# Masked running sum taken at one row per batch, then a matrix product: lengths read into registers, and the sum moved to fp32 matmuls in four column groups

## The chip, the cores and the metric

One core of a Trainium2 chip runs the kernel. The metric is device time in microseconds (us) for one execution. Three runs of the kernel before gave 200.6, 201.1 and 201.49 us; the median is 201.1 us.

## What is computed

```python
B, S, D = 8, 8192, 512                     # x [B,S,D] fp32, lengths [B] int64, w [D,D] fp32
mask = (pos < lengths[:, None, None])
cs = np.cumsum(x * mask, axis=1)
mid_features = cs[np.arange(B), lengths // 2, :]
return np.matmul(mid_features[:, None, :], w).squeeze(1)
```

Only one row of each running sum is used, the one at `lengths // 2`. So for each batch the answer is the sum of the first n rows of x, n = min(lengths // 2 + 1, lengths), multiplied by w. The inputs are drawn once with a fixed seed. The lengths are 1138, 5379, 511, 4113, 1809, 7542, 7716 and 1140, so n is 570, 2690, 256, 2057, 905, 3772, 3859 and 571 for batches 0 to 7: 14,680 rows of 2 KB in all. Since lengths are below 8192, n is never above 4096 = S/2.

## The kernel before, in words

The kernel doesn't know the lengths when it is built, so it loads the first 4096 rows of every batch: 8 x 4096 rows of 2 KB, 67.1 MB. For each batch there are 8 groups, each of 4 x 128 rows. A group is one DMA of 1 MB issued by SP into `xt` (L65), in which every partition receives four separate rows of 2 KB, 128 rows apart. VectorE casts the group to bf16 in `xb` (L67), and TensorE adds it with four matmuls (L70), whose stationary operand is one column of `mask_t`: 1 for rows at or before the middle, 0 for the others. All 32 x 8 = 256 matmuls add into one row of PSUM per batch, which VectorE copies to `mf_sb` (L72). The pool `sb` has 12 buffers for each of the two tiles.

The masks are made at the start: SP loads the lengths (L41), VectorE halves them (L43, L46), GpSimd broadcasts them over the partitions (L48) and writes row numbers (L51), and VectorE compares (L55).

Behind the last batch stands a chain: the eight sums lie in one partition, so they are written to DRAM (L75) and read back transposed with eight DMAs of 4-byte elements (L78); four fp32 matmuls multiply them by w (L85), VectorE copies the result (L88) and SP writes it (L89). The order on each engine is the order of the program, and the Tile framework sets the semaphores. SP's queue holds all of the transfers in this order: lengths, the 64 groups of x, the round trip, with the four loads of w among them, and the output.

Of the kernel before, what the change touches and what calls it, by code (L numbers as in the profile page):

```python
# [1 line left out]

# [4 lines left out]


@with_exitstack
def kernel(  # L10
    ctx: ExitStack,
    tc: tile.TileContext,
    x: bass.AP,
    lengths: bass.AP,
    w: bass.AP,
    out: bass.AP,
):
    nc = tc.nc
    import concourse.bass as _b
    _b.log.warn_once_per_call_stack = lambda *a, **k: None  # L20
    ctx.enter_context(nc.allow_non_contiguous_dma(reason="meta"))
    B, S, D = x.shape
    assert D == 512 and B == 8
    SM = S // 2
    NCH = SM // 128
    G = 4
    NGRP = NCH // G

    f32 = mybir.dt.float32
    bf16 = mybir.dt.bfloat16  # L30
    f32r = mybir.dt.float32r
    i32 = mybir.dt.int32

    sb = ctx.enter_context(tc.tile_pool(name="sb", bufs=12))
    sc = ctx.enter_context(tc.tile_pool(name="sc", bufs=1))
    pp = ctx.enter_context(tc.tile_pool(name="pp", bufs=4, space=bass.MemoryType.PSUM))
    dp = ctx.enter_context(tc.tile_pool(name="dp", bufs=1, space=bass.MemoryType.DRAM))

    lens_i = sc.tile([1, 2 * B], i32)
    lsrc = lengths.tensor.reshape([B]).bitcast(i32).ap().rearrange("(o t) -> o t", o=1)  # L40
    nc.sync.dma_start(out=lens_i[:, :], in_=lsrc)  # L41
    mid_i = sc.tile([1, B], i32)
    nc.vector.tensor_scalar(out=mid_i[:], in0=lens_i[:, ::2], scalar1=1, scalar2=None,  # L43
                            op0=mybir.AluOpType.logical_shift_right)
    mid_f = sc.tile([1, B], f32)
    nc.vector.tensor_copy(out=mid_f[:], in_=mid_i[:])  # L46
    mid_bc = sc.tile([128, B], f32)
    nc.gpsimd.partition_broadcast(mid_bc[:], mid_f[:])  # L48

    iota_t = sc.tile([128, NCH], f32)  # L50
    nc.gpsimd.iota(iota_t[:], pattern=[[128, NCH]], base=0, channel_multiplier=1,  # L51
                   allow_small_or_imprecise_dtypes=True)
    mask_t = sc.tile([128, B, NCH], bf16)
    for b in range(B):
        nc.vector.tensor_scalar(out=mask_t[:, b, :], in0=iota_t[:],  # L55
                                scalar1=mid_bc[:, b:b + 1], scalar2=None,
                                op0=mybir.AluOpType.is_le)

    mf_sb = sc.tile([1, B, D], f32)
    xr = x.rearrange("b (ng g p) d -> b ng p g d", p=128, g=G)  # L60
    for b in range(B):
        ps = pp.tile([1, D], f32, tag="ps")
        for ng in range(NGRP):
            xt = sb.tile([128, G, D], f32, tag="xt")
            nc.sync.dma_start(out=xt[:], in_=xr[b, ng])  # L65
            xb = sb.tile([128, G, D], bf16, tag="xb")
            nc.vector.tensor_copy(out=xb[:], in_=xt[:])  # L67
            for g in range(G):
                c = ng * G + g
                nc.tensor.matmul(out=ps[:], lhsT=mask_t[:, b, c:c + 1], rhs=xb[:, g, :],  # L70
                                 start=(c == 0), stop=(c == NCH - 1))
        nc.vector.tensor_copy(out=mf_sb[:, b, :], in_=ps[:])  # L72

    mf_dram = dp.tile([1, B, D], f32)
    nc.sync.dma_start(out=mf_dram[:], in_=mf_sb[:])  # L75
    mf_t = sc.tile([128, 4, B], f32)
    for b in range(B):
        nc.sync.dma_start(out=mf_t[:, :, b],  # L78
                          in_=mf_dram[:, b, :].rearrange("o (kc p) -> (o p) kc", p=128))

    ps_out = pp.tile([B, D], f32)
    for kc in range(4):
        wt = sb.tile([128, D], f32)
        nc.sync.dma_start(out=wt[:], in_=w[kc * 128:(kc + 1) * 128, :])
        nc.tensor.matmul(out=ps_out[:], lhsT=mf_t[:, kc, :], rhs=wt[:],  # L85
                         start=(kc == 0), stop=(kc == 3))
    out_sb = sc.tile([B, D], f32)
    nc.vector.tensor_copy(out=out_sb[:], in_=ps_out[:])  # L88
    nc.sync.dma_start(out=out[:], in_=out_sb[:])  # L89


# [1 line left out]
_INS = ['x', 'lengths', 'w']  # L93
_OUTS = [((8, 512), 'float32')]


# [23 lines left out]
```

## Time and profile before

| | |
|---|---|
| Median of three runs | 201.1 us (200.6 to 201.49) |
| Span of the profiled execution, first to last instruction | 200.5 us; no other time of that execution is recorded |
| TensorE matmul, weight load | 113.9 us (57%), 29.1 us (14%) busy |
| VectorE | 85.4 us busy (43%) |
| Bytes moved by DMA | 68.26 MB, mean 340 GB/s |
| Mean granted TensorE clock | 0.625 of full speed |

The profile's page lists the span in 40 slices of about 5 us; a digit is the busy share of a slice in tenths. In the rows below, PE is TensorE's matmul and PEld its weight load, DVE is VectorE, POOL is GpSimd, SPq is SyncE's queue of DMA issues. The chain that ended last is followed back from the last instruction to whatever released each step.

### The profile page before, as it was taken

The numbers are of one execution on the slowest core, as the hardware profiler recorded it, in microseconds if no ns is written. First come the engines' busy times: TensorE is split into PE (matmuls) and PEld (weight loads), VectorE is DVE, ScalarE is ACT, GpSimd is POOL, SyncE is SP. The second block draws the span as 40 slices with busy tenths as digits, with TensorE's granted clock in tenths as the row PEclk, the third lists the DMA queues.
The fourth block names the chain that finished last, engine by engine and source line by source line (L and its number), as shares of the span: only waits on it lengthen the run. The fifth ranks groups of instructions, "written<-read, shape, count | busy, mean of one in ns | idle before, by whom it ended". The sixth has DMA issues, their size and how long they took to land.

```text
span 200.5 us, 853 instructions
## 1 busy us (share of the span) xinstructions
PE 113.9 (57%) x264; PEld 29.1 (14%) x264; DVE 85.4 (43%) x83; POOL 0.6 (0%) x6
## 2 busy tenths in 40 slices
PE   0004947766653756677655665764867765663093
PEld 0001311111110111111111111111211111110010
DVE  0334664344644444443644454445544364441001
POOL 0000000000000000000000000000000000000000
PEclk9999995555588555555585558555555558555558
DMA  4999999999999999999999999999999999980400
GB/s 148 367 398 386 387 387 388 387 386 386 386 389 388 385 388 386 386 386 386 386 387 386 387 387 387 386 387 388 386 386 387 384 387 386 388 312 9 3 0 3
DMA packets 38616, 68.26 MB, mean 340 GB/s; under 512 B 5323, under 2 KB 5323, under 8 KB 38611
## 3 DMA queue, kind: packets, MB, share of 16 engines
q1 hardware_dynamic: 38612, 68.21, 93.5%
q8 instruction: 2, 0.03, 0.1%
q14 instruction: 2, 0.02, 0.0%
HBM read 68.17 MB, written 0.03 MB: 340 GB/s over the span
## 4 chain that ended last, share of the span: by engine, by line
DMA 78%; SPq 11%; PE 5%; DVE 3%; issue 1%; DVEq 0%
DMA xt<-in_x_dram 76%; SPq L65 9%; PE ps_out L85 3%; DVE xb L67 2%; PE ps L70 2%; SPq L78 2%; DMA mf_t<-mf_dram 1%; DMA mf_dram<-mf_sb 1%; DVE mf_sb L72 0%; DVE out_sb L88 0%; SPq L41 0%; DVEq L67 0%
## 5 line engine op out<-in xcount | busy, mean ns | idle before, releaser
L70 PE MATMUL ps<-xb,mask_t 128*1 128x512 bf16 x256 | 107.4, 575 | 74.7 <-DVE xb L67 56.8
L67 DVE CAST xb<-xt 128x2048 bf16<-128x2048 f32 x64 | 78.2, 1224 | 77.2 <-DMA xt<-in_x_dram 77.2
L70 PEld LDWEIGHTS <-mask_t 128*1 128x1 bf16 x256 | 28.1, 110 | 153.0 <-issue 130.1
L72 DVE COPY mf_sb<-ps 1x512 f32<-1x512 f32 x8 | 5.4, 679 | 14.8 <-PE ps L70 14.8
L85 PE MATMUL ps_out<-wt,mf_t 128*8 128x512 f32 x8 | 6.6, 1000 | 8.8 <-DMA mf_t<-mf_dram 8.8
L88 DVE COPY out_sb<-ps_out 8x512 f32<-8x512 f32 x1 | 0.7, 679 | 14.7 <-PE ps_out L85 14.7
L55 DVE TENSOR_SCALAR mask_t<-iota_t,mid_bc 128x32 bf16<-128x32 f32 x8 | 1.3, 236 | 4.0 <-POOL mid_bc L48 4.0
L85 PEld LDWEIGHTS ps_out<-wt,mf_t 128*8 128x8 f32 x8 | 0.9, 126 | 14.0 <-issue 14.0
L43 DVE TENSOR_SCALAR mid_i<-lens_i 1x8 int32<-1x8 int32 x1 | 0.2, 159 | 1.9 <-DMA lens_i<-in_lengths_dram 1.9
L48 POOL PARTITION_BROADCAST mid_bc<-mid_f x1 | 0.3, 280 | 8.2 <-issue 8.2
L51 POOL IOTA iota_t<- 128x32 f32 x1 | 0.2, 157 | 8.5 <-issue 8.5
L46 DVE CAST mid_f<-mid_i 1x8 f32<-1x8 int32 x1 | 0.2, 159 | 0.0
L104 POOL MEMSET const-uint8-127<- 128x1 uint8 x1 | 0.1, 102 | 0.0
L104 POOL MEMSET const-bfloat16-1.0<- 128x1 bf16 x1 | 0.1, 101 | 0.0
L104 POOL MEMSET const-float32-0.0<- 128x1 f32 x1 | 0.1, 98 | 0.2 <-issue 0.2
L104 POOL MEMSET const-float32-1.0<- 128x1 f32 x1 | 0.1, 98 | 0.0
## 6 DMA issues: line engine op xcount, KB each, us to landing
xt<-in_x_dram SPq DMA_DIRECT2D x64, 1024.0 KB, 14.4
wt<-in_w_dram SPq DMA_DIRECT2D x4, 256.0 KB, 10.8
mf_t<-mf_dram SPq DMA_DIRECT2D x8, 2.0 KB, 2.3
lens_i<-in_lengths_dram SPq DMA_DIRECT2D x1, 0.1 KB
mf_dram<-mf_sb SPq DMA_DIRECT2D x1, 16.0 KB
out_dram<-out_sb SPq DMA_DIRECT2D x1, 16.0 KB
```

What stands on the lines that cost most here:

```text
L43: nc.vector.tensor_scalar(out=mid_i[:], in0=lens_i[:, ::2], scalar1=1, scalar2=None, op0=mybir.AluOpType.logical_shift_right)
L46: nc.vector.tensor_copy(out=mid_f[:], in_=mid_i[:])
L48: nc.gpsimd.partition_broadcast(mid_bc[:], mid_f[:])
L55: nc.vector.tensor_scalar(out=mask_t[:, b, :], in0=iota_t[:], scalar1=mid_bc[:, b:b + 1], scalar2=None, op0=mybir.AluOpType.is_le)
L65: nc.sync.dma_start(out=xt[:], in_=xr[b, ng])
L67: nc.vector.tensor_copy(out=xb[:], in_=xt[:])
L70: nc.tensor.matmul(out=ps[:], lhsT=mask_t[:, b, c:c + 1], rhs=xb[:, g, :], start=(c == 0), stop=(c == NCH - 1))
L72: nc.vector.tensor_copy(out=mf_sb[:, b, :], in_=ps[:])
L78: nc.sync.dma_start(out=mf_t[:, :, b], in_=mf_dram[:, b, :].rearrange("o (kc p) -> (o p) kc", p=128))
L85: nc.tensor.matmul(out=ps_out[:], lhsT=mf_t[:, kc, :], rhs=wt[:], start=(kc == 0), stop=(kc == 3))
L88: nc.vector.tensor_copy(out=out_sb[:], in_=ps_out[:])
L104: nc = _bacc.Bacc("TRN2", target_bir_lowering=False, num_devices=1)
```

## The change

The kernel is written anew, without the Tile framework's semaphores, between one set of hand-placed waits. SP and TensorE each load the lengths into 16 registers and work out n for every batch (`counts`). Both then walk the same code: for every batch up to eight whole blocks of 512 rows, each behind a comparison of n with a constant (`whole_blocks`), so that a block beyond n is neither loaded nor added. The rows left over, fewer than 512, are split by the binary digits of n: 256 rows, 128 rows, and the last up to 127 rows, for which 32, 64, 96 or 128 rows are loaded and those beyond n masked. With the lengths drawn there are 26 whole blocks; three loads of 256 rows (batches 2, 4, 6), three of 128 (1, 4, 5), and seven last ones (32 rows for batches 1, 3, 4 and 6, 64 for 0, 5 and 7): 39 loads of 14,784 rows, 30.28 MB. The first 26 carry 27.26 MB, the 13 others 3.01 MB.

In a block each partition now takes four neighbouring rows, one run of 8 KB. There is no cast: TensorE multiplies fp32 directly, and of the four row sets of a block each goes to its own 32-column group of the array, `tile_position=(0, 32*j)`, with eight stationary columns of which one is 1, so that batch b's sum is added to row b of the group. Afterwards the four groups are added (`fold`) by four matmuls which also transpose the sums, in place of the round trip through DRAM, and the product with w is split over the four column groups by output columns. The lengths for the masks and all of w are loaded by ACT's queue at the start. `xt` holds two batches (b % 2) of eight blocks; before SP loads over a block it waits for TensorE to have read it (`wait_free`).

```diff
+    xt = sb("xt", [P, 2, NB, G, D])
+    rem = sb("rem", [P, B, G, D])
...
+    def counts(eng):
+        regs = [eng.alloc_register(f"n_{eng.engine.name}_{i}") for i in range(2 * B)]
+        eng.load(regs, lens_words)
+        for b in range(B):
+            length, n = regs[2 * b], regs[2 * b + 1]
+            eng.reg_alu(n, length, 1, ALU.logical_shift_right)
+            eng.reg_alu(n, n, 1, ALU.add)
+            eng.reg_alu(n, n, length, ALU.min)
+        return regs[1::2], regs[0]
+
+    def whole_blocks(eng, n, body, k=0):
+        if k < NB:
+            with eng.If_cmp(n, BLK * (k + 1), "IS_GE"):
+                body(k)
+                whole_blocks(eng, n, body, k + 1)
...
+    @block.sync
+    def _(sp):
+        ns, t = counts(sp)
+        def wait_free(b, k):
+            if b >= 0:
+                with sp.If_cmp(ns[b], BLK * (k + 1), "IS_GE"):
+                    sp.wait_ge(s_free[b], k + 1)
+                with sp.Else():
+                    wait_free(b - 2, k)
+        for b in range(B):
+            def load_block(k):
+                wait_free(b - 2, k)
+                sp.dma_start(
+                    out=xt[:, b % 2, k],
+                    in_=x[b, k * BLK:(k + 1) * BLK].rearrange("(p g) d -> p g d", g=G),
+                ).then_inc(s_full[b][k], 16)
+            whole_blocks(sp, ns[b], load_block)
...
+        sp.wait_ge(s_pool, 1)
+        for b in range(B):
+            sp.reg_alu(t, ns[b], 256, ALU.bitwise_and)
+            with sp.If_cmp(t, 1, "IS_GE"):
+                sp.reg_alu(base, ns[b], ~(2 * 256 - 1), ALU.bitwise_and)
+                sp.dma_start(
+                    out=rem[:, b, 0:2],
+                    in_=rows(b, base, 256).rearrange("(p g) d -> p g d", g=2),
+                ).then_inc(s_rem[b][0], 16)
...
+        sp.wait_ge(s_dve, DVE_MASK + 3)
+        for j in range(0, 4, 2):
+            sp.dma_start(out=out[:, j * P:(j + 1) * P], in_=o_sb[32 * j:32 * j + B]).then_inc(s_out, 16)
+        sp.wait_ge(s_out, 64)
+    @block.scalar
+    def _(act):
+        act.dma_start(out=lens[:], in_=lens_words.to_broadcast((P, 2 * B))).then_inc(s_len, 16)
+        act.dma_start(out=wt[:], in_=w.rearrange("(kc p) d -> p kc d", p=P)).then_inc(s_w, 16)
...
+    @block.tensor
+    def _(pe):
+        ns, t = counts(pe)
+        def add(j, weights, rows):
+            return pe.matmul(s_ps[32 * j:32 * j + weights.shape[-1]], lhsT=weights, rhs=rows,
+                             start=False, stop=False, skip_group_check=True,
+                             tile_position=(0, 32 * j))
+        for j in range(4):
+            pe.matmul(s_ps[32 * j:32 * j + 32], lhsT=zero[:, :32], rhs=zero[:],
+                      start=True, stop=False, skip_group_check=True, tile_position=(0, 32 * j))
+        for b in range(B):
+            one = sel[:, B - 1 - b:2 * B - 1 - b]
+            def add_block(k):
+                pe.wait_ge(s_full[b][k], 16)
+                for j in range(G):
+                    mm = add(j, one, xt[:, b % 2, k, j])
+                mm.then_inc(s_free[b], 1)
+            whole_blocks(pe, ns[b], add_block)
...
+            with pe.If_cmp(t, 1, "IS_GE"):
+                pe.wait_ge(s_rem[b][2], 16)
+                add(3, mask[:, b], rem[:, b, 3])
+        for j in range(4):
+            mm = pe.matmul(s_ps[32 * j:32 * j + 32], lhsT=zero[:, :32], rhs=zero[:],
+                           start=False, stop=True, skip_group_check=True,
+                           tile_position=(0, 32 * j))
+        mm.then_inc(s_pe, 1)
+        pe.wait_ge(s_dve, DVE_MASK + 1)
+        for kc in range(KC):
+            mm = pe.matmul(mf_ps[:, kc * B:(kc + 1) * B], lhsT=s_sb[:, kc * P:(kc + 1) * P],
+                           rhs=fold[:], start=True, stop=True)
...
+        for kc in range(KC):
+            for j in range(4):
+                mm = pe.matmul(o_ps[32 * j:32 * j + B, :P], lhsT=mf_sb[:, kc],
+                               rhs=wt[:, kc, j * P:(j + 1) * P],
+                               start=(kc == 0), stop=(kc == KC - 1), tile_position=(0, 32 * j))
```

## Rows read from the trace of the kernel before

**Rows 1.** The page's 40 slices: clock, DMA share, rate.
```profile
PEclk9999995555588555555585558555555558555558
DMA  4999999999999999999999999999999999980400
GB/s 148 367 398 386 387 387 388 387 386 386 386 389 388 385 388 386 386 386 386 386 387 386 387 387 387 386 387 388 386 386 387 384 387 386 388 312 9 3 0 3
```

**Rows 2.** The page: the chain that ended last, by line.
```profile
DMA xt<-in_x_dram 76%; SPq L65 9%; PE ps_out L85 3%; DVE xb L67 2%; PE ps L70 2%; SPq L78 2%; DMA mf_t<-mf_dram 1%; DMA mf_dram<-mf_sb 1%; DVE mf_sb L72 0%; DVE out_sb L88 0%; SPq L41 0%; DVEq L67 0%
```

**Rows 3.** The page: groups (count, busy us, mean ns, idle before).
```profile
L70 PE MATMUL ps<-xb,mask_t 128*1 128x512 bf16 x256 | 107.4, 575 | 74.7 <-DVE xb L67 56.8
L67 DVE CAST xb<-xt 128x2048 bf16<-128x2048 f32 x64 | 78.2, 1224 | 77.2 <-DMA xt<-in_x_dram 77.2
```

**Rows 4.** The chain in order of time, from the last group on (start, us).
```profile
178.86 0.04 issue
178.90 1.24 DVE xb L67
180.14 0.04 issue
180.18 1.88 PE ps L70 x4
...
182.79 1.67 DMA mf_dram<-mf_sb
...
184.47 0.39 SPq L78
...
188.21 2.29 DMA mf_t<-mf_dram
190.50 0.38 issue
190.88 6.57 PE ps_out L85 x8
197.44 0.02 issue
197.47 0.68 DVE out_sb L88
```

**Rows 5.** Stretches: length, PE, PEld, DVE, POOL busy, clock, DMA share, GB/s.
```profile
2.00:3.00 1.00, 0.00 (x0) 0.00 (x0) 0.26 (x2) 0.00 (x0) 1.00 0.26 80
40.00:160.00 120.00, 76.18 (x176) 19.68 (x176) 56.51 (x49) 0.00 (x0) 0.56 1.05 387
184.50:190.50 6.00, 0.00 (x0) 0.00 (x0) 0.00 (x0) 0.00 (x0) 0.50 0.37 3
```

**Rows 6.** The tile xt: SP's issues and time to landing.
```profile
L65 SPq DMA_DIRECT2D xt<-in_x_dram x64: 407/2535/4254, 1.1 to 164.4; - x64
DMA to landing us min/median/max: 5.4/14.4/15.8
```

**Rows 7.** Timeline of the start and of the output (start, us).
```profile
0.73 0.34 SPq L41 DMA_DIRECT2D lens_i<-in_lengths_dram  x1
1.13 1.50 SPq L65 DMA_DIRECT2D xt<-in_x_dram  x3
1.95 0.16 DVE L43 TENSOR_SCALAR mid_i<-lens_i 1x8 int32<-1x8 int32 x1 [1.95 <-DMA lens_i<-in_lengths_dram]
...
198.18 0.30 SPq L89 DMA_DIRECT2D out_dram<-out_sb  x1
```

**Rows 8.** Line L85, fp32 on TensorE (ns min/median/max, first and last start).
```profile
L85 PEld LDWEIGHTS ps_out<-wt,mf_t x8: 88/138/138, 190.8 to 195.9; 128*8 128x8 f32 x8
L85 PE MATMUL ps_out<-wt,mf_t x8: 630/1061/1061, 190.9 to 196.8; 128*8 128x512 f32 x8
L85 PEldq EVENT_SEMAPHORE  x4: 51/51/51, 190.1 to 190.8; - x4
```

**Rows 9.** More stretches, columns as in rows 5, for TensorE's clock.
```profile
17.90:22.50 4.60, 4.60 (x11) 1.33 (x12) 4.35 (x10) 0.00 (x0) 1.00 1.05 386
22.90:25.90 3.00, 3.00 (x16) 1.16 (x14) 1.26 (x2) 0.00 (x0) 1.00 1.05 386
31.00:44.00 13.00, 8.93 (x21) 2.19 (x20) 6.13 (x5) 0.00 (x0) 0.50 1.05 387
190.90:197.40 6.50, 6.50 (x8) 0.90 (x8) 0.00 (x0) 0.00 (x0) 0.54 0.00 0
```

**Rows 10.** Timeline: two weight loads of the fp32 product.
```profile
191.68 0.14 PEld L85 LDWEIGHTS ps_out<-wt,mf_t 128*8 128x8 f32 x1 [0.71 <-issue]
192.54 0.14 PEld L85 LDWEIGHTS ps_out<-wt,mf_t 128*8 128x8 f32 x1 [0.72 <-issue]
```

**Rows 11.** The page: DMA queues that fetch instructions.
```profile
q8 instruction: 2, 0.03, 0.1%
q14 instruction: 2, 0.02, 0.0%
```

More of the change, by code (lines that the diff above doesn't have):

```diff
@@ L4 @@
 import concourse.tile as tile
-from concourse import bass_utils, mybir
+from concourse import mybir
 from concourse._compat import with_exitstack
+F32 = mybir.dt.float32
+I32 = mybir.dt.int32
+ALU = mybir.AluOpType
+ds = bass.ds
+P = 128
 @with_exitstack
@@ L18 @@
     nc = tc.nc
-    import concourse.bass as _b
-    _b.log.warn_once_per_call_stack = lambda *a, **k: None
-    ctx.enter_context(nc.allow_non_contiguous_dma(reason="meta"))
+    ctx.enter_context(nc.allow_non_contiguous_dma(reason="lengths"))
     B, S, D = x.shape
-    assert D == 512 and B == 8
-    SM = S // 2
-    NCH = SM // 128
     G = 4
[L27 to L86, printed above, removed]
@@ L87, with sb @@
-    out_sb = sc.tile([B, D], f32)
-    nc.vector.tensor_copy(out=out_sb[:], in_=ps_out[:])
-    nc.sync.dma_start(out=out[:], in_=out_sb[:])
+    BLK = P * G
+    NB = S // 2 // BLK
+    KC = D // P
+    STEP = 32
+    xf = x.rearrange("b s d -> (b s) d")
+    lens_words = lengths.tensor.reshape([B]).bitcast(I32).ap().rearrange("(o t) -> o t", o=1)
+    ctx.enter_context(tc.tile_critical(no_gpsimd_drain=True))
+    def sb(name, shape, dt=F32):
+        return ctx.enter_context(nc.sbuf_tensor(name, shape, dt))
@@ new lines, in ps, with sem @@
+    def ps(name, shape):
+        return ctx.enter_context(nc.psum_tensor(name, shape, F32))
+    def sem(name):
+        return tc.alloc_semaphore(name)
+    xt = sb("xt", [P, 2, NB, G, D])
+    rem = sb("rem", [P, B, G, D])
+    wt = sb("wt", [P, KC, D])
+    lens = sb("lens", [P, 2 * B], I32)
+    cnt = sb("cnt", [P, B], I32)
+    cap = sb("cap", [P, B], I32)
+    row = sb("row", [P, 1], I32)
+    mask = sb("mask", [P, B, B])
+    sel = sb("sel", [P, 2 * B - 1])
+    zero = sb("zero", [1, D])
@@ new lines @@
+    fold_i = sb("fold_i", [P, B], I32)
+    fold = sb("fold", [P, B])
+    s_sb = sb("s_sb", [P, D])
+    mf_sb = sb("mf_sb", [P, KC, B])
+    o_sb = sb("o_sb", [P, P])
+    s_ps = ps("s_ps", [P, D])
+    mf_ps = ps("mf_ps", [P, D])
+    o_ps = ps("o_ps", [P, D])
+    s_full = [[sem(f"full{b}_{k}") for k in range(NB)] for b in range(B)]
+    s_rem = [[sem(f"rem{b}_{k}") for k in range(3)] for b in range(B)]
+    s_free = [sem(f"free{b}") for b in range(B)]
+    s_w, s_len, s_out = sem("w"), sem("len"), sem("out")
@@ new lines @@
+    s_pool, s_dve, s_pe = sem("pool"), sem("dve"), sem("pe")
+    def counts(eng):
[12 more added lines that the diff above has]
+                whole_blocks(eng, n, body, k + 1)
@@ new lines, in _ @@
+    @block.scalar
+    def _(act):
+        act.dma_start(out=lens[:], in_=lens_words.to_broadcast((P, 2 * B))).then_inc(s_len, 16)
+        act.dma_start(out=wt[:], in_=w.rearrange("(kc p) d -> p kc d", p=P)).then_inc(s_w, 16)
+        act.wait_ge(s_dve, DVE_MASK + 3)
+        for j in range(1, 4, 2):
+            act.dma_start(out=out[:, j * P:(j + 1) * P], in_=o_sb[32 * j:32 * j + B]).then_inc(s_out, 16)
+    @block.gpsimd
+    def _(pool):
+        pool.memset(rem[:, :, 3], 0.0).then_inc(s_pool, 1)
+        pool.iota(row[:], pattern=[[0, 1]], base=0, channel_multiplier=1)
+        pool.iota(fold_i[:], pattern=[[-1, B]], base=128, channel_multiplier=1).then_inc(s_pool, 1)
@@ new lines, in _, with step @@
+    @block.vector
+    def _(dve):
+        done = 0
+        def step(do, *args, **kw):
+            nonlocal done
+            if done:
+                dve.wait_ge(s_dve, done)
+            do(*args, **kw).then_inc(s_dve, 1)
+            done += 1
+        step(dve.memset, zero[:], 0.0)
+        step(dve.memset, sel[:], 0.0)
+        step(dve.memset, sel[:, B - 1:B], 1.0)
+        assert done == DVE_SEL
+        step(dve.memset, mask[:], 0.0)
+        step(dve.memset, o_ps[:, :P], 0.0)
+        dve.wait_ge(s_len, 16)
+        step(dve.tensor_scalar, out=cnt[:], in0=lens[:, ::2], scalar1=1, scalar2=None,
+             op0=ALU.logical_shift_right)
+        step(dve.tensor_scalar, out=cap[:], in0=cnt[:], scalar1=1, scalar2=None, op0=ALU.add)
+        step(dve.tensor_tensor, out=cnt[:], in0=cap[:], in1=lens[:, ::2], op=ALU.min)
+        step(dve.tensor_scalar, out=cap[:], in0=cnt[:], scalar1=127, scalar2=None,
+             op0=ALU.bitwise_and)
+        dve.wait_ge(s_pool, 2)
+        step(dve.tensor_tensor, out=mask[:].rearrange("p a b -> p (a b)")[:, ::B + 1], in0=cap[:],
+             in1=row[:].to_broadcast((P, B)), op=ALU.is_gt)
+        step(dve.tensor_scalar, out=cnt[:], in0=fold_i[:], scalar1=31, scalar2=None,
+             op0=ALU.bitwise_and)
+        step(dve.tensor_scalar, out=fold[:], in0=cnt[:], scalar1=0, scalar2=None, op0=ALU.is_equal)
+        assert done == DVE_MASK
+        dve.wait_ge(s_pe, 1)
+        step(dve.tensor_copy, out=s_sb[:], in_=s_ps[:])
+        dve.wait_ge(s_pe, 2)
+        step(dve.tensor_copy, out=mf_sb[:].rearrange("p a b -> p (a b)"), in_=mf_ps[:, :KC * B])
+        dve.wait_ge(s_pe, 3)
+        step(dve.tensor_copy, out=o_sb[:], in_=o_ps[:, :P])
```

40 lines of the change are left out of this document (added).

## The prediction

> **What bounds the kernel now.** I read the page's slices first. From the second 5 us to the 35th slice the DMA engines are busy throughout at 384 to 398 GB/s [rows 1]; 120 us from the middle read 387 GB/s, while TensorE and VectorE have idle time in the same stretch [rows 5]. The chain agrees: 76% of the span is the load of x and 9% SP's queue at the same loads [rows 2], and both engines behind it wait: the casts for DMA, the matmuls for the casts [rows 3]. So the time is bytes over rate: 67.1 MB at 387 GB/s are 173.4 us. Data first flows at about 2.74 us (the share of 0.26 in the third microsecond, [rows 5]), 1.6 us after the first issue [rows 7], and the last group has landed at 178.86 us [rows 4]: 2.7 us more than rate alone gives, for the ramps. Behind it stand 21.6 us of tail to the end of the span at 200.5 us: cast, matmuls, round trip through DRAM, product, output [rows 4].
>
> All sums are made against that span; the median of the runs is 0.6 us above it, and I add that at the end.
>
> **The stream of x.** It falls from 67.1 to 30.28 MB. At the old rate this takes 78.2 us. The packets change too: a partition's share of a block is one run of 8 KB instead of four of 2 KB, which the trace doesn't show. At 387 GB/s over 16 engines a packet of 2 KB takes 84.7 ns. The round trip moves 8 x 512 elements of 4 bytes in 6 us at a DMA share of 0.37 [rows 5]: 0.37 x 16 x 6 us / 4096 = 8.7 ns each, nearly all of it cost per packet, so an upper bound of that cost. Three such costs saved make 8 KB in 4 x 84.7 - 3 x 8.7 = 313 ns, or 419 GB/s. The ends are 387 and 419; I take 410 for the 27.26 MB of whole blocks, nearer the top because the small packet is a direct row for the overhead, and 387 for the 3.01 MB of shorter rows: 66.5 + 7.8 = 74.3 us (73 to 78).
>
> Here a rule speaks against any such rate. The Trainium skill, "DMA: Bandwidth & Descriptors", section "Where 436 GB/s comes from", says that for transfers between HBM and SBUF a limit of about 358 GB/s per core binds; by it the stream would take 84.6 us and the sum would be 10 us higher. The trace contradicts it, with 387 GB/s held for 120 us.
>
> **The start.** Before the first load of x, SP now reads 16 registers from DRAM, works out eight n with 24 register operations, and compares once. No row shows a register load. The lower end is one small transfer, from the issue of the lengths at 0.73 us to VectorE's use at 1.95 us: 1.2 us [rows 7]; the upper end is one such trip for each of 16 words, 19 us. It is one instruction over 64 contiguous bytes, so nearest the single trip: 1.2 us and 16 writes of 0.05 us (a semaphore instruction took 51 ns, [rows 8]) make 2.0. The operations at 0.05 us make 1.2, the comparison 0.1. The first issue of x comes at 0.7 + 2.0 + 1.2 + 0.1 = 4.0 us instead of 1.13. The Trainium skill, "Runtime: NRT & Kernel Launch", section "Instruction fetch mechanics", gives about 200 ns for each register loaded; the sum would be 1.2 us higher by that.
>
> The other preparation costs nothing on the path: w and the broadcast lengths leave ACT's queue in the first microseconds, while x hasn't begun (w's 1 MB at 387 GB/s is 2.7 us, which is what it costs if x starts at once). The masks on VectorE and GpSimd are first needed after the whole blocks. The casts, 78.2 us of VectorE [rows 3], go, but they lay beside DMA.
>
> **TensorE beside the stream.** An fp32 matmul of 512 columns is two MATMUL records [rows 8], 0.86 us apart [rows 10] at a granted clock of 0.54 [rows 9], the lower level: 1.72 us at 1.2 GHz, half at 2.4 GHz. A block has four: 6.88 us in a row at 1.2 GHz, 1.72 if the four column groups run fully beside each other. A block arrives every 1.05 MB / 410 GB/s = 2.56 us. No row shows column groups. The second record of one group needs its own weights, while the first of the next group needs other columns, so I take half, neighbours overlapping in pairs: 3.44 us at 1.2 GHz, 1.72 at 2.4. The first is too slow, but then TensorE is never idle, and the trace shows what follows: a run of matmuls without a gap was at 0.42 us each for 4.6 us and then at 0.19 [rows 9]. So TensorE lags by a few blocks, speeds up, and catches up; where it idles in each period it falls back to 0.50 [rows 9]. A lag delays DMA only when SP finds a buffer unread: the nearest case is the seventh block loaded (batch 3), which waits for the second, so four blocks or 10 us of lag are free. In SP's queue everything later stands behind that wait.
>
> The 13 loads of remainders are 13 issues of 0.5 us (as at L78: eight from 184.47 to 188.21 us, [rows 4]) plus 24 tests of 0.1 us: 9 us. They are hidden: SP runs about five groups ahead (14.4 us to landing, [rows 6]) when it comes to them. Without this cover they would exceed their 7.8 us of data by 1.2.
>
> **The tail**, from the last landing:
> - TensorE's lag with the last matmul: 0.9 us (one matmul at 2.4 GHz) to 9.6 (16 remainder matmuls and the last block at 1.2 GHz and half overlap, less 7.8 us of arrival); I take 2.5.
> - Four closing matmuls: 0.9 to 6.9, taken 1.7; the copy of the sums 0.7, as L88 [rows 4].
> - The fold, eight short records: 0.09 each (a short weight load, [rows 8]) to 0.43 (256 columns' worth, half of rows 10): 0.7 to 3.4; I take 1.5, its columns being eight. A small copy 0.2 [rows 7].
> - The product with w, as many columns as before but in four groups: 0.8 (a quarter, at 2.4 GHz) to 6.6 (as before, [rows 4]); I take half, 3.3. Copy 0.3.
> - Output: 2.3 us from issue to the span's end before [rows 7], one more issue of 0.55 on the queue: 2.85. Handoffs 0.4.
>
> Together 13.45 us, in place of 21.6.
>
> **Sum.** 4.0 + 1.6 + 74.3 + 2.7 = 82.6 us to the last landing, 96.1 with the tail, 96.7 with the 0.6: **97 us**.
>
> **Rivals.**
> *The column groups don't overlap, at the high clock.* For it: in the old product each weight load starts only as the matmul before it ends (0.86 us apart, [rows 10]), and no row shows two matmuls side by side. Against it: those all use the same columns. All four matmuls of a block then take 3.44 us at 2.4 GHz, more than DMA's 2.56, and TensorE is the bound: 26 blocks and 16 remainder matmuls are 30 blocks' worth, 103.2 us, from the first landing at 4.0 + 5.4 [rows 6], with 2.3 us for the slow first 4.6 us and 12.7 us of tail: 128 us. The Trainium skill, "TensorE: Matmul & The Clock Gate", Part 3, says that weight loads overlap matmuls in flight only when the row group differs, and here all use all rows; that rule would make this rival true. The same part reports a gain of 2.38 for three column tiles, which would not.
>
> *The same at the low clock: slower than before.* If matmuls one after another also stay at 1.2 GHz, the 30 blocks' worth cost 206.4 us, the tail 19.5, from 9.4 us: 236 us. It decides from 5.7 us for four matmuls on: (201.1 - 0.6 - 9.4 - 19.5) / 30. For it: 6.5 us of fp32 without a gap stayed at about 0.54 [rows 9]. Against it: the 4.6 us row rose.
>
> *Jumps cost instruction fetches.* Before, the program ran straight and two queues fetched twice each [rows 11]. Each batch ends its blocks with a jump over those skipped. If each of TensorE's eight jumps waits for a fetch that takes as long as the quickest load of x, 5.4 us [rows 6], that is 43 us: 9.4 + 51.6 + 43 + 12.7 + 0.6 = 117 us. The Trainium skill's runtime page, same section, says that a taken branch which leaves the fetched pages stalls for a fetch. By that a few jumps at most would stall: a jump is forward over little code, much of it fetched next anyway.
>
> *The stream doesn't shrink*, because skipped loads are issued after all: about 190 us. The comparisons stand around the loads; I see no way to it.
>
> **How the numbers follow.** Chances: the forecast 0.70, no overlap at the high clock 0.16, fetches 0.07, no overlap at the low clock 0.05, no shrinking 0.02. All lower ends at once (419 GB/s, registers 1.2, tail 7.75) give 89 us. At the upper ends, 387 GB/s adds 4, the long tail 17, registers read one by one 17; they hardly meet. 90 to 124 us takes in most of the forecast, the fetches and part of a partial overlap, and leaves out the full 128 and the 236. The runs' spread is about 0.45%, so 0.5% is what can be told from no change. Faster 0.94, within 0.5% 0.01, slower 0.05.
>
> **What would show it.** Right: about 31 MB moved; 400 to 420 GB/s in the middle; the first load of x issued near 4 us and DMA busy to about 82 us; matmuls of neighbouring groups starting less than 0.86 us apart (0.43 at the high clock) on average; TensorE waiting for DMA in the blocks; no x in the last 14 us. Wrong: SP waiting for TensorE with DMA idle, or TensorE busy throughout (no overlap); gaps at batch ends that neither semaphore nor DMA explains (fetches); a first issue beyond 6 us (registers).

## The result, and the profile after

The changed kernel takes 100.91 us, the median of five runs (100.47 to 102.44), where the kernel before took 201.49 us on the same chip: a ratio of 0.5007, 95% interval 0.4984 to 0.503. The forecast was 97 us, 90 to 124.

The execution shown below is the longest of the five, 102.44 us with a span of 100.6; a second profile (in the experiments, `again`) took 101.11 us with a span of 99.3, and the table below has both. Some 1.8 us lie outside the span, where the prediction had added 0.6.

The page's slices (2.5 us each now) and the DMA queues, to stand beside [rows 1, 11]:

```profile
PEclk9999999998555699755999555596555569998555
DMA  0836999999999999999999999999999995100000
GB/s 2 270 148 195 427 427 430 430 420 420 427 420 417 427 423 417 414 417 414 427 420 420 423 423 423 410 420 423 420 281 290 328 283 136 34 0 0 0 7 0
q8 instruction: 5, 0.08, 0.3%
q14 instruction: 5, 0.04, 0.1%
HBM read 31.33 MB, written 0.02 MB: 312 GB/s over the span
```

Three things differ from before. DMA is busy early, with w, and then idle for parts of two slices (shares of 0.3 and 0.6, 148 and 195 GB/s). The blocks run at 410 to 430 GB/s. And from the 30th slice on, with all DMA engines still busy, the rate falls to some 290: there the rest rows are loaded.

The groups, in place of [rows 3] (count, busy us, mean ns, idle before):

```profile
L218 PE MATMUL s_ps<-xt,sel 128*8 128x512 f32 x208 | 42.6, 905 | 28.6 <-DMA xt<-in_x_dram 23.4
L218 PEld LDWEIGHTS s_ps<-xt,sel 128*8 128x8 f32 x208 | 3.7, 91 | 67.5 <-DMA xt<-in_x_dram 58.0
```

26 blocks of eight records are the 208; TensorE waits for DMA between them, 23.4 of the 28.6 us for which it is idle there. The chain in order of time shows SP's first 8 us (start, us, what):

```profile
0.96 0.86 SPq L80
1.82 0.04 issue
1.86 4.20 SPq L80
6.06 0.04 issue
6.10 0.27 SPq L83
...
7.20 0.42 SPq L113
```

L80 is the register load: an address first, then 16 words in 4.20 us. The first x is issued at 7.20 us. The end, in the same view:

```profile
90.53 1.03 PE s_ps L254 x8
91.59 0.70 DVE s_sb L182
92.34 1.71 PE mf_ps L261 x8
94.07 0.20 DVE mf_sb L182
94.32 1.94 PE o_ps L268 x32
96.28 0.29 DVE o_sb L182
```

And TensorE's timeline: the weight loads and matmuls of a block at 22.55 us (granted clock 1.00, the higher level), the matmuls of one at 25.03 us (0.50, the lower level), three blocks behind a gap, and the last wait that the view puts down to a landing:

```profile
22.55 0.12 PEld L218 LDWEIGHTS s_ps<-xt,sel 128*8 128x8 f32 x8 [2.83 <-DMA xt<-in_x_dram]
22.55 1.04 PE L218 MATMUL s_ps<-xt,sel 128*8 128x512 f32 x8 [1.30 <-DMA xt<-in_x_dram]
...
25.03 1.90 PE L218 MATMUL s_ps<-xt,sel 128*8 128x512 f32 x8 [1.43 <-DMA xt<-in_x_dram]
...
42.27 5.55 PE L218 MATMUL s_ps<-xt,sel 128*8 128x512 f32 x24 [2.71 <-issue]
...
88.51 0.10 PEld L218 LDWEIGHTS s_ps<-rem,mask 128*8 128x8 f32 x2 [0.55 <-DMA rem<-in_x_dram]
```

The last landing is taken from the trace's landing events, of which every load leaves 16.

| Step | Predicted | Execution shown | `again` |
|---|---|---|---|
| First issue of x | 4.0 us | 7.20 | 7.11 |
| First bytes of x | 5.6 | about 8.5 | about 8.3 |
| Rate in the blocks | 410 GB/s | 420 | 421 |
| A block on TensorE, low / high clock | 3.44 / 1.72 us | 1.90 / 1.04 | 1.90 / 1.04 |
| Last landing | 82.6 us | 88.3 | 88.1 |
| Tail to the end of the span | 13.45 | 12.3 | 11.2 |
| Outside the span | 0.6 | 1.8 | 1.8 |

### The profile page after: what moved, and what is told of

Its sections match the earlier page's. It is cut to its first block, busy times and chain, and to the rows that moved or that the text cites. A ratio compares the mean times of both kernels' runs of the same rounds, so it can differ in the third digit from the quotient of the medians.

```text
span 100.6 us, 1017 instructions
## 1 busy us (share of the span) xinstructions
PE 58.3 (58%) x296; PEld 8.3 (8%) x296; DVE 3.9 (4%) x15; POOL 4.0 (4%) x7
## 3 DMA queue, kind: packets, MB, share of 16 engines
q10 hardware_dynamic: 704, 1.07, 3.2%
## 4 chain that ended last, share of the span: by engine, by line
DMA 41%; SPq 31%; issue 13%; PE 9%; DVE 1%
DMA xt<-in_x_dram 25%; DMA rem<-in_x_dram 16%; SPq L113 10%; SPq L143 6%; SPq L80 5%; PE s_ps L218 5%; SPq L129 3%; PE o_ps L268 2%; PE mf_ps L261 2%; SPq L105 1%; SPq L136 1%; PE s_ps L254 1%; SPq L90 1%; DVE s_sb L182 1%; SPq L121 1%
## 5 line engine op out<-in xcount | busy, mean ns | idle before, releaser
L218 PE MATMUL s_ps<-xt,sel 128*8 128x512 f32 x208 | 42.6, 905 | 28.6 <-DMA xt<-in_x_dram 23.4
L218 PEld LDWEIGHTS s_ps<-xt,sel 128*8 128x8 f32 x208 | 3.7, 91 | 67.5 <-DMA xt<-in_x_dram 58.0
L218 PE MATMUL s_ps<-rem,mask 128*8 128x512 f32 x14 | 8.0, 670 | 0.8 <-issue 0.8
L218 PE MATMUL s_ps<-rem,sel 128*8 128x512 f32 x18 | 6.6, 643 | 0.1
L224 PE MATMUL s_ps<-zero 1*32 1x512 f32 x8 | 1.9, 1056 | 7.3 <-issue 7.3
L169 POOL MEMSET rem<- 128x4096 f32 x1 | 3.5, 3512 | 0.5 <-SPq L40 0.5
L261 PE MATMUL mf_ps<-fold,s_sb 128*128 128x8 f32 x8 | 1.7, 340 | 0.8 <-DVE s_sb L182 0.8
L268 PE MATMUL o_ps<-wt,mf_sb 128*8 128x128 f32 x32 | 1.9, 416 | 0.3 <-DVE mf_sb L182 0.3
L261 PEld LDWEIGHTS mf_ps<-fold,s_sb 128*128 128x128 f32 x8 | 1.6, 298 | 1.7 <-DVE s_sb L182 1.7
L268 PEld LDWEIGHTS o_ps<-wt,mf_sb 128*8 128x8 f32 x32 | 1.1, 126 | 0.7 <-DVE mf_sb L182 0.4
L254 PE MATMUL s_ps<-zero 1*32 1x512 f32 x8 | 1.1, 600 | 0.0
```

The source lines that it names most:

```text
L169: pool.memset(rem[:, :, 3], 0.0).then_inc(s_pool, 1)
L218: return pe.matmul(s_ps[32 * j:32 * j + weights.shape[-1]], lhsT=weights, rhs=rows, start=False, stop=False, skip_group_check=True, tile_p ...
L224: pe.matmul(s_ps[32 * j:32 * j + 32], lhsT=zero[:, :32], rhs=zero[:], start=True, stop=False, skip_group_check=True, tile_position=(0, 32 ...
L254: mm = pe.matmul(s_ps[32 * j:32 * j + 32], lhsT=zero[:, :32], rhs=zero[:], start=False, stop=True, skip_group_check=True, tile_position=(0 ...
L261: mm = pe.matmul(mf_ps[:, kc * B:(kc + 1) * B], lhsT=s_sb[:, kc * P:(kc + 1) * P], rhs=fold[:], start=True, stop=True)
L268: mm = pe.matmul(o_ps[32 * j:32 * j + B, :P], lhsT=mf_sb[:, kc], rhs=wt[:, kc, j * P:(j + 1) * P], start=(kc == 0), stop=(kc == KC - 1), t ...
```

## The experiments

Ratios are to the kernel before, with the 95% interval. A difference between two experiments is called shown where their intervals don't meet.

### Do the column groups matter?

```diff
         def add(j, weights, rows):
+            j = 0
```

> All row sets of a block are added in the first column group, so that no two matmuls of a sum use different columns; nothing else changes. Theory 1 (the groups run beside each other only because they use different columns): a block takes 6.9 us at 1.2 GHz and 3.4 at 2.4, more than DMA's 2.5; TensorE is busy throughout at the high clock, 30 blocks' worth or 103 us from the first landing at 12 us, and the tail: 130 us. Theory 2 (TensorE overlaps them anyway, or has time to spare): 101 us. Were the clock to stay low: 235 us.

Measured: 127.21 us in one run, span 125.4. TensorE never waits (window view: PE, PEld, DVE, POOL busy, clock, DMA share, GB/s), and each weight load stands 0.43 us behind the one before, as in [rows 10] but at the high clock:

```profile
20.00:60.00 40.00, 40.00 (x95) 8.39 (x94) 0.00 (x0) 0.00 (x0) 1.00 0.93 354
60.00:100.00 40.00, 40.00 (x95) 8.44 (x94) 0.00 (x0) 0.00 (x0) 1.00 0.78 288
```
```profile
59.98 0.09 PEld L219 LDWEIGHTS s_ps<-xt,sel 128*8 128x8 f32 x1 [0.34 <-issue]
60.41 0.09 PEld L219 LDWEIGHTS s_ps<-xt,sel 128*8 128x8 f32 x1 [0.34 <-issue]
```

Theory 1 holds. In one group the time of the prediction's first rival comes out, 127 for a predicted 128; with four groups the eight records of a block take 1.04 us where 3.44 stand one behind the other. The column groups are what keeps TensorE off the path. The granted clock also reads 1.00 in both stretches, in which TensorE never idles.

### What is the larger packet worth?

```diff
-  in_=x[b, k * BLK:(k + 1) * BLK].rearrange("(p g) d -> p g d", g=G),
+  in_=x[b, k * BLK:(k + 1) * BLK].rearrange("(g p) d -> p g d", g=G),
```

> In a block each partition again takes four rows of 2 KB, 128 rows apart, instead of one run of 8 KB; only the order of the sum changes. Theory 1 (the cost per packet sets the rate): the 27.26 MB of blocks go at 387 instead of 424 GB/s, 6.1 us more: 107 us. Theory 2 (the higher rate comes from something else, such as the missing casts): 101 us.

Measured: 106.95 us, ratio 0.5281 (0.526 to 0.5302), 6.1 us more than `again` (100.86, below). The same window of `runs_2k` and then of `again`:

```profile
20.00:60.00 40.00, 25.47 (x116) 2.05 (x120) 0.00 (x0) 0.00 (x0) 0.81 1.05 386
```
```profile
20.00:60.00 40.00, 23.55 (x128) 1.90 (x120) 0.00 (x0) 0.00 (x0) 0.74 1.01 421
```

Theory 1 holds: 386 GB/s, the old rate, comes back with the old runs. Packets of 8 KB took 312 ns (median) in the middle of `again`, against the 313 worked out from 4-byte packets in the prediction.

### How much is the rows, how much the rest?

```diff
+    N = [4096] * 8
+    def whole_blocks(eng, n, body):
+        for k in range(n // BLK):
+            body(k)
...
-            whole_blocks(sp, ns[b], load_block)
+            whole_blocks(sp, N[b], load_block)
```

> No lengths in registers and no jumps: 4096 rows of every batch are loaded and added in 64 whole blocks; it leaves out the lengths altogether, and the sums are of 4096 rows each. All else as in the changed kernel. Theory 1 (the rows set the time, and the rest of the change is the larger packets and the shorter tail): 67.1 MB at 422 GB/s are 159 us, data from 4 us on, 3 us of spread, 12 us of tail: 178 us. Theory 2 (the new structure, buffers and fp32 matmuls, can't keep up over 64 blocks): 200 us and more.

Measured: 182.71 us in one run. The middle and the end of its stream:

```profile
20.00:100.00 80.00, 51.34 (x256) 3.83 (x256) 0.00 (x0) 0.00 (x0) 0.72 1.01 421
...
166.00:168.00 2.00, 1.42 (x12) 0.12 (x8) 0.00 (x0) 0.00 (x0) 0.50 0.26 107
168.00:170.00 2.00, 1.44 (x12) 0.12 (x8) 0.00 (x0) 0.00 (x0) 0.50 0.03 12
```

Theory 1 holds, though 4.7 us short of the measurement: TensorE keeps up over 64 blocks, at 421 GB/s for 80 us. So about 19 of the 100.5 us are gained by packets and tail (201.4 to 182.7), and 82 by loading only the rows that count. The 82 are net: `all_rows` has neither a register load nor rest rows.

### The start

> The changed kernel once more, to stand beside the next three on the same chip: 100.9 us, first load of x issued at 7.2 us, last load of x landed 88 to 89 us after the start.

Measured: 100.86 us, 0.5015 (0.4978 to 0.5051).

```diff
-        eng.load(regs, lens_words)
+        for b, v in enumerate([1138, 5379, 511, 4113, 1809, 7542, 7716, 1140]):
+            eng.reg_mov(regs[2 * b], v)
```

> SP and TensorE take the eight lengths from constants moved into registers instead of loading 16 registers from DRAM; it leaves out the reading of the lengths by these two engines, all branches stay. The load took 5.1 us at L80, and x would be issued at about 2.5 us instead of 7.2. Theory 1 (DMA's idle time decides): w's load fills DMA from 2.7 to 6 us already, so only the idle 2.4 us up to x's first bytes come back: 98.5 us. Theory 2 (the first issue decides): the whole 4.7 us come back: 96.2 us. Theory 3 (the end is set by the late engine and by the rest rows, not by the start): 100.9 us.

Measured: 98.71 us, 0.4893 (0.4868 to 0.4917). x is issued at 2.52 us, and 2.15 us come back, nearly theory 1's 2.4. The register load puts x 4.7 us later, but w is loaded meanwhile, so only DMA's idle time counts. In the changed kernel that is the share missing in these two rows, behind w, 2.4 us in all:

```profile
6.00:8.00 2.00, 0.68 (x4) 0.21 (x8) 0.00 (x0) 0.00 (x0) 1.00 0.04 16
8.00:10.00 2.00, 1.25 (x8) 0.00 (x0) 0.00 (x0) 0.00 (x0) 1.00 0.76 246
```

Next, two blocks ahead of the load:

```diff
+        for b in range(2):
+            sp.dma_start(
+                out=xt[:, b, 0],
+                in_=x[b, :BLK].rearrange("(p g) d -> p g d", g=G),
+            ).then_inc(s_full[b][0], 16)
         ns, t = counts(sp)
...
             def load_block(k):
+                if b < 2 and k == 0:
+                    return
```

> SP issues the first block of batches 0 and 1 before it loads the registers, and skips them in the walk; nothing else changes. Theory 1 (DMA's idle time decides): DMA has two blocks and w, 7.4 us of work, from about 2.7 us on and no gap before the walk's first loads at 8.5 us: 98.2 us. Theory 2 (the first issue decides): 94.8 us, all of the 6.1 us. Theory 3 (the start is not on the path): 100.9 us.

Measured: 100.33 us, 0.4985 (0.4962 to 0.5008), no difference that can be told from `again`. What I had not reckoned with stands on the line of the register load, in `spec2`:

```profile
L80 SPq TENSOR_LOAD <-in_lengths_dram_ptr x1: 3382/3382/3382, 1.9 to 1.9; - x1
...
L80 SPq TENSOR_LOAD <-in_lengths_dram x1: 4659/4659/4659, 5.3 to 5.3; - x1
```

Beside transfers, address and words took 8.0 us in place of 5.0. The third block was issued at 11.47 us, and DMA ran short again (share 0.84 and 0.75 from 10 to 14 us). Theory 1's price for DMA's idle time isn't refuted by that, since the idle time didn't go.

### Jumps and instruction fetches

`straight` has the eight counts as numbers in the program, so comparisons, jumps and register loads are gone (one of many such places):

```diff
-            with pe.If_cmp(t, 1, "IS_GE"):
+            if N[b] & 256:
                 pe.wait_ge(s_rem[b][0], 16)
```

> The row counts are built in as numbers: no register load, no comparison, no jump, and a program a third as long; it leaves out that the lengths are read for the counts. Same loads, same matmuls, same waits. Theory 1 (instruction fetches of 16 KB ride on one DMA engine and put it behind the others by about 1.1 us each, and every landing waits for the slowest engine): the start gives back 2.8 us as DMA has no gap, and the spread between the first and the last engine of a landing, 3.3 us at the end of the blocks, falls to about 1: 95 us. Theory 2 (the spread comes from the loads themselves): only the start, 98 us. Theory 3 (jumps stall TensorE or SP on the path): below 94 us.

Measured: 97.45 us, 0.4838 (0.481 to 0.4866). That is 3.4 us less than `again` and 1.3 less than `mov_regs`, near theory 2's 98. x is issued at 0.96 us. Theory 1 had its sign from the trace: the times at which the 16 engines finish one landing lie closely together until an instruction fetch of 16 KB runs on one of them. These are landings of `again` and of `straight`, from the trace's landing events; the spread is the time from the first to the last of the 16, in us:

```
again:     landing at 27.3 us, spread 0.7   fetch of 16 KB at 28.5 us, 1.09 us long
           landing at 30.8 us, spread 1.7
straight:  landing at 36.4 us, spread 2.2   fetch of 16 KB at 37.4 us, 1.07 us long
           landing at 39.7 us, spread 3.0
           last of the blocks' steady part, 69.5 us, spread 3.0 (again: 71.7 us, 2.9)
```

In these two places the spread grows by 1.0 and 0.8 us, as if the fetch put one engine back. It doesn't always: the fetches at 39.4 and 45.1 us in `again` leave the spread at 1.7. And `straight` starts with a spread of 2.2 us before any fetch, and ends where `again` ends. So the program's length isn't shown to cost time here, and theory 1 falls; where `straight`'s first 2.2 us come from stays open.

The jumps: in the execution shown, TensorE's timeline has two gaps that the view puts down to "issue", 2.44 us before 31.84 us and 2.71 us before 42.27 us (row above for the second). Each lies beside a fetch of q8, at 29.33 and 39.58 us:

```profile
27.51 1.89 PE L218 MATMUL s_ps<-xt,sel 128*8 128x512 f32 x7 [0.59 <-DMA xt<-in_x_dram]
31.84 3.63 PE L218 MATMUL s_ps<-xt,sel 128*8 128x512 f32 x17 [2.44 <-issue]
```
```profile
L90 PEldq COMPARE_BRANCH  x34: 64/64/3556, 7.4 to 78.6; - x34
```

The first gap lies inside a block: seven of its eight matmul records run at 27.51 us, the eighth only at 31.84, 1.9 us after the next block has landed (29.95). A jump isn't shown to cause it. The second stands at the end of batch 4, where one comparison with its jump (L90, ns min/median/max) took 3.56 us on TensorE's queue. The next block landed only at 40.95 us, so 1.3 us of that gap are TensorE's own delay. `again` has only the second, 1.4 us behind the landing. `straight` has neither: its fetch at 37.4 us held nothing up, and the block that landed at 39.70 us was begun at 39.75. That fetches cause the delays fits this and the five fetches of q8 (two before, [rows 11]), but isn't shown apart from the jumps. DMA stayed busy through both gaps (the slices above), and TensorE caught up: three blocks without a pause, at 42.27 us.

### The rest rows

The last load of each batch takes 32 or 64 rows, over as many partitions. Now 128 over all:

```diff
-                load_last(0, 128)
+                sp.dma_start(out=rem[:, b, 3], in_=rows(b, base, 128)).then_inc(s_rem[b][2], 16)
```

> Each batch's last load takes 128 rows over all 128 partitions instead of 32 or 64 rows over as many partitions; rows beyond n stay masked. 1.18 MB more are loaded. In the changed kernel the rate falls from 420 to about 290 GB/s while the rest rows are loaded, with all engines busy. Theory 1 (loads into few partitions slow the writes): the rest, now 4.19 MB, runs at about 400 GB/s: 99.5 us. Theory 2 (packets of 2 and 4 KB are slow by themselves, or the addresses from registers are): 1.18 MB more at 290 GB/s, 4 us: 105 us.

Measured: 99.15 us, 0.494 (0.4917 to 0.4962): faster than `again` by 1.7 us, with 1.18 MB more. The same ten microseconds in `again`, then in `full128`:

```profile
72.00:82.00 10.00, 6.46 (x29) 0.84 (x22) 0.00 (x0) 0.00 (x0) 0.67 1.03 305
```
```profile
72.00:82.00 10.00, 6.86 (x36) 1.00 (x28) 0.00 (x0) 0.00 (x0) 0.82 1.02 393
```

DMA is as busy in both and moves 305 GB/s in one and 393 in the other. The packets say why: in this window those of 2 KB took 116 ns on average in `again` and 86 in `full128`, those of 4 KB 232 and 168. Not only the small loads are slow: the 4 KB packets belong to loads of 256 rows over all partitions. Theory 1 holds in that the shape of these loads, and not the packets' size or the addresses from registers, sets the rate. The last landing comes 0.8 us earlier (87.25 us for 88.07) although 1.18 MB more are loaded, 3.0 us at 393 GB/s, so the shape had cost the stream about 3.8 us, an estimate. The edit makes each of these loads wider and larger at once; which of the two counts isn't told apart by any run. The Trainium skill, "SBUF — State Buffer", section "Door 1: The DMA port swizzle", says that partitions 0 to 31 and 0 to 63 alike reach only eight of SBUF's 16 DMA ports. By that rule loads into them are slower; that they also slow what shares their ports is my inference. The packet times above agree with both, though the trace doesn't show ports.

The engines also finish further and further apart. In `again` the 16 events of a landing lie within 0.3 us at 14.5 us, 2.9 at 71.7 us and up to 5.2 in the rest rows (3.2 in `full128`), so that DMA is nearly idle before the last landing:

```profile
84.00:86.00 2.00, 2.00 (x10) 0.30 (x8) 0.00 (x0) 0.00 (x0) 1.00 0.24 79
86.00:88.00 2.00, 1.79 (x8) 0.30 (x8) 0.00 (x0) 0.00 (x0) 1.00 0.09 29
```

Now the same loads in another place:

```diff
-        for b in range(B):
+        for b in range(6):
             def load_block(k):
...
             with sp.If_cmp(t, 1, "IS_GE"):
                 load_last(0, 128)
+        for b in range(6, B):
+            def load_block(k):
```

> SP issues and TensorE adds the rest rows between the blocks of batch 5 and those of batch 6, so that the last eight loads are whole blocks. Same loads. Theory 1 (the rest loads cost the same wherever they stand): the stream ends as late, 88 us, TensorE has one matmul group less behind it: 100.5 us. Theory 2 (they cost because they stand last, with nothing behind to keep the engines that are ahead busy): the spread of up to 5 us between engines is no longer waited for by small loads: 97 us.

Measured: 103.14 us, 101.16 to 103.55, without an interval. Where the rest rows now stand, and where blocks follow:

```profile
54.00:64.00 10.00, 7.37 (x32) 1.04 (x24) 0.00 (x0) 0.00 (x0) 0.66 1.06 288
```
```profile
70.00:84.00 14.00, 7.68 (x41) 0.60 (x40) 0.00 (x0) 0.00 (x0) 0.76 1.01 421
```

The slow stretch has moved with the rest rows, at 288 GB/s, and the blocks behind it run at 421. Theory 2's 97 us is excluded; the cost goes with the loads, not with their place, as theory 1 has it. The shortest run is 0.7 us above theory 1's 100.5; the others spread too widely for a ratio, and why stays open.

### Towards a faster version

```diff
-        eng.load(regs, lens_words)
+        eng.load(regs[::2], lens_words[:, ::2])
```

> SP and TensorE load only the eight low words of the lengths, every second one, instead of all 16 words; the upper words are zero and unused. In the changed kernel the register load took 0.86 us for the address and 4.2 us for 16 registers. Theory 1 (it costs by the register, 0.26 us each): 2.1 us, first load of x issued at 5.1 us, and DMA's idle time after w shrinks from 2.4 to about 0.3 us: 98.8 us. Theory 2 (it costs by the instruction): 100.9 us.

Measured: 102.92 us, 0.5116 (0.5093 to 0.5139), slower than `again`. Both theories fall on one row:

```profile
L80 SPq TENSOR_LOAD <-in_lengths_dram x1: 5612/5612/5612, 2.0 to 2.0; - x1
```

Eight separate words take 5.6 us, 0.70 each; 16 neighbouring ones took 4.1 to 4.2. x is issued at 8.76 us. So half the words, apart, cost more than all of them side by side. Among neighbouring words the number counts as well, as the last kernel below shows.

The same line together with `full128`'s:

> The eight-register load together with last loads of 128 rows over all partitions. If the two gains add (2.1 us at the start, 1.7 at the end): 97.1 us. If the second only shows when the first doesn't: 99 us.

Measured: 101.24 us, 0.5033 (0.501 to 0.5056). The two parts add, 2.1 us lost and 1.7 gained; of the expectation's two gains, the first had the wrong sign.

The last kernel keeps words together and loads them in two parts, with the full loads for the rest:

```diff
-        ns, t = counts(sp)
...
+        def read(first, last):
+            sp.load(regs[2 * first:2 * last], lens_words[:, 2 * first:2 * last])
...
+        read(0, 2)
...
         for b in range(B):
+            if b == 2:
+                read(2, B)
...
```

> SP first loads only the four words of the lengths of batches 0 and 1, issues their six blocks, and then loads the other twelve words while those blocks are under way; last loads take 128 rows over all partitions. TensorE's load is as in the changed kernel. Theory 1 (neighbouring words cost about 0.26 us each, as 16 did in 4.1 us): the first load takes about 1.1 us, x is issued at about 3.3 us, the second load is covered by 15 us of transfers, and the 2.2 us that constants in registers saved add to the gain of the full loads: 97.0 us. Theory 2 (a load costs the same for any number of words, or the second one stalls the walk under DMA traffic): 99 us or more.

Measured: 96.41 us, 0.4814 (0.4791 to 0.4837), faster than the changed kernel, than `mov_regs` and than `full128`. SP's part of the chain at the start:

```profile
2.12 1.63 SPq L104
...
7.39 3.99 SPq L104
...
11.51 5.54 SPq L104
```

Four words take 1.63 us, and the first x is issued at 4.16. The second load is slow beside transfers, 3.99 and 5.54 us, but six blocks cover it: from the third slice of its page (4.7 us) on the rate is 409 to 440 GB/s, up to one dip to 378. The idle time after w is gone.

## Why the prediction was right, and by which steps it was off

**The mechanism held.** The time is bytes over rate. 30.28 MB instead of 67.1, TensorE beside it, a shorter tail: DMA is busy from the first block to the rest rows and TensorE waits for it, as forecast, and `all_rows` puts the rows' share at 82 of the 100.5 us. The measured 100.9 lie 3.9 us above the predicted 97. For the profile of `again`, 101.1 against 96.7, the terms differ so:

- *The start*, "1.2 us and 16 writes of 0.05 us make 2.0": mis-sized. Address and words took 4.98 us (5.06 in the execution shown), and first bytes came at 8.3 instead of 5.6, +2.7. A first issue beyond 6 us was the prediction's own sign of being wrong on the registers, and it came at 7.1. The step went to the row of one small transfer, but words are not free once the trip is paid. By the Trainium skill, "Runtime: NRT & Kernel Launch", section "Instruction fetch mechanics", cited there, about 200 ns a register would have given an estimate of 3.2 us for the 16; 0.26 us a word were measured side by side and 0.70 apart. And w, "2.7 us if x starts at once", covers half of the delay: taking the load out gave 2.15 us (`mov_regs`).
- *The rate in the blocks*, 410: 420 measured, 386 with the old packets (`runs_2k`). The 8.7 ns per packet were the right term, and the upper end, 419, would have been the better choice: -1.7 us on 27.26 MB. The limit of about 358 GB/s that the Trainium skill states in "DMA: Bandwidth & Descriptors", section "Where 436 GB/s comes from", weighed there, is contradicted once more, by 421 GB/s over 40 us.
- *The rest rows*, 7.8 us "at 387 GB/s": the term that was furthest off. From first bytes to the last landing 79.8 us passed where 77.0 (74.3 and 2.7 of ramps) had been summed, +2.8, though the blocks took 1.7 less. So rest rows and ramps together cost some 4.5 us more than priced. I took the rate of a full load for loads over 32 and 64 partitions. `full128` shows that this shape slows the packets beside it, and about 3.8 us are estimated from it; 1.7 us come back in the time, although it loads more. The remaining 0.7 us isn't tied to a cause; the engines' growing distance is a candidate. By the rest rows two of the prediction's signs of being right were missed: DMA busy to about 82 us, and no x in the last 14.
- *The tail*, 13.45: 11.2, -2.2. The product took 1.5 us for 3.3, as the four groups overlap, the closing matmuls 1.06 for 1.7, the fold 1.07 for 1.5; the output, 4.0 us from its issue at 95.30 to the span's end, took 1.15 more. In the execution shown the tail is 1 us longer: fold and product took 1.71 and 1.94 us (rows above), with the granted clock at 0.56 and 0.50 there, where `again` had 1.00 for the fold and 0.67 for the product.
- *Outside the span*: 1.8 instead of 0.6, +1.2. The profiled execution of before has no time of its own, so the median of other executions was no measure of it. In the runs beside `again` the kernel before has 201.2 us with a span of 199.4, also 1.8.

So the sum came within 4 us partly by luck: errors of +2.7, +4.5 and +1.2 us stand against -1.7 and -2.2. And the range up to 124 us was set by the rivals, so lying in it says little about the terms.

**TensorE**, taken at half overlap, overlaps fully: eight records in 1.90 us at the low clock, where 1.72 was the lower end. With either value TensorE stays off the path (by the prediction's account through catching up at the high clock), so the error moved nothing but the tail. The Trainium skill's rule in "TensorE: Matmul & The Clock Gate", Part 3, that weight loads overlap only between different row groups, doesn't hold here: the eight weight loads of the block at 22.55 us, all over all rows, are a single burst of 0.12 us beside its matmuls. The gain of 2.38 for three column tiles, which it also reports, points the right way: here four take 1.04 us for 3.44, a gain of 3.3.

**The rivals.** No overlap at the high clock: right in price (128, and 127.2 for `one_group`), wrong in its condition. The low clock: even without overlap it stayed high (granted clock 1.00, `one_group`). Fetches: at most two delays of 1.9 and 1.3 us on TensorE, in place of eight of 5.4, and covered. The second stands at a batch's end, where the prediction had put its sign of fetches. That the remainder issues are hidden held as well: SP issued the last at 75.97 us, while blocks were still landing.

## What to carry to other kernels

Price a load by its shape as well as its bytes: a small one over a quarter or half of the partitions can slow the full ones beside it, and padding it to all 128 was cheaper here than leaving bytes out. A value that branches need is read at the very start; read only the neighbouring words that the first transfers need, and the others behind them. Column groups make four thin fp32 matmuls cost hardly more than one (1.04 us for 0.86), which let this kernel drop the casts.

## What the runs showed that I had not expected

- A register load depends on the words' places: 4.1 us for 16 side by side, 5.6 for eight apart, 1.6 for four side by side; and on traffic: address and words 8.0 us beside transfers instead of 5.0 (`spec2`).
- A 16 KB instruction fetch occupies one DMA engine for about 1.1 us, and behind some fetches, not all, the landings stay spread by about that much more.
- Small loads over few partitions slow packets of other loads, 4 KB from 168 to 232 ns, with DMA showing as fully busy.
- The 16 DMA engines drift apart, from 0.3 us near the start of the stream to 4 or 5 in the rest rows (`again`), and the last landing waits for the last of them. Only a part of this is traced to a cause.
